# One program order over all stages, the second pass of a turn before its first down product, and another order of refill

## The chip, the cores and the metric

The kernel runs on one core of a Trainium2 chip. The metric is the device time of one execution in microseconds; lower is better. The input is fixed: 256 tokens, two layers.

## The reference

Each of the two layers does a token mixer and then a mixture of experts, both behind a root-mean-square norm and both added to the residual stream. Layer 0 mixes with differential attention, layer 1 with latent attention. The mixture picks for each token one group of eight and in it two of its eight experts; 64 experts per layer, each with three float32 matrices of 1024 x 256 or 256 x 1024 (1.049 MB each):

```python
for i in range(DEPTH):                       # 2
    h = rms_norm(x, attn_norm[i])
    x = x + (diff_attention if i == 0 else mla_attention)(h, ...)
    h = rms_norm(x, ffn_norm[i])
    x = x + hier_moe(h, ...)

def body(e, acc):                            # e = 0 .. 63
    hid = jax.nn.silu(t @ w_gate[e]) * (t @ w_up[e])
    return acc + combine[:, e, None] * (hid @ w_down[e])
```

## The kernel before

A layer is an attention stage (`diff_attention`, `latent_attention`), a front that norms, routes and sorts (`Front`), and the expert stage (`moe`). In the two attention stages and their fronts the instructions are written as named steps, and the strings `ORDER0` and `ORDER1` give the order in which they are issued.

The expert stage goes in 16 turns (0 to `LAST` = 15) of four experts. TensorE multiplies the four experts side by side, 32 columns each, so a pass has room for 32 tokens per expert (`SLOTS`). A pass consists of: the selection of tokens (`places`, DVE L1262), the gather by matrix products with the selection (`step`, TensorE L1270; `gained`, DVE L334), gate and up (`into`, `gate_up`, L1323), SiLU on ACT (L1328) and the product with up on DVE (L1330), the hidden columns transposed (L1335) and copied (ACT L1337), down (`out_of`, `down`, L1349), a copy out of PSUM (`taken`, L1381), and back (L1389), which spreads the rows over the tokens and adds them to `xs` (L1354). The weighted selection is transposed for it (`turned`, L1291). The product back of turn t is done in turn t + 1.

Where an expert has more than 32 tokens in a turn, the turn is full and takes a second pass. A word of bits, `path`, computed by the front, says which turns are full: `full` tests it (L1449, one If per turn, on every engine) and `second` is the body. Inside it, a further If (L1406) leads to `long_way`, for more than 64 tokens, which this input does not need. On this input three turns are full: turns 1 and 15 of layer 0 and turn 11 of layer 1.

Before, the If stands at the end of a turn, behind down, `taken` and the weighting for the next turn.

Weights pass through ten rooms of 2.1 MB. A unit of load is the gate and up of one expert (two DMAs), or the down matrices of two experts (two DMAs); three units per pair of experts, six per turn. Unit n lies in room n mod 10 of a ring (`RING`), so unit n + 10 can be loaded when unit n has been read for the last time. `load_unit` issues the DMAs on SP's queue, in the order of the list `order`; `free` marks units as read and issues the loads at the head of the list as long as their rooms are marked. The gate/up units are marked inside the If (in each of its branches), the down units behind it. SP issues in order, and each DMA waits there for the last reader of its room.

The planner keeps the written order of an engine's instructions only inside a `manual_schedule` region. Before, there are four such regions for TensorE, ACT and DVE: attention and front of layer 0 (`start`), the expert stage of layer 0, attention and front of layer 1 (`all_manual`), the expert stage of layer 1. What lies between two regions (`rope_tables` for layer 1, L264 to L267) and the order across an edge are the planner's. SP is in written order throughout.

TensorE's sequencer can be told ahead that a branch will probably be taken (`mark_branch_hint_location`): each If of a turn that is not full carries a hint for the If of the next turn. `preferred_fallthrough_block=True` puts the body of the If behind the branch, so that a turn that is not full jumps over `second`.

```python
order = list(range(ROOMS, 96 + 2 * ROOMS))
order[2:8] = order[3], order[4], order[2], order[6], order[7], order[5]
```

Of the kernel before, what the change touches and what calls it, by code (L numbers as in the profile page):

```python
# [10 lines left out]
F32R = mybir.dt.float32r  # L11
# [4 lines left out]
OP = mybir.AluOpType  # L16
# [53 lines left out]
def trunk_kernel(  # L70
# [14 lines left out]
    def psum_bank():  # L85
        return psum.tile([128, 512], F32, name="bank", bufs=8)
# [6 lines left out]
    def temp(cols):  # L93
        return work.tile([128, 512], F32, name="temp", bufs=3)[:, 0:cols]
# [140 lines left out]

    start = ctx.enter_context(ExitStack())
    start.enter_context(tc.manual_schedule(engines={e.engine for e in (PE, ACT, DVE, POOL, SP)}))
    ones_b = consts.tile([128, 128], BF, name="ones_b")
# [47 lines left out]
    def rsqrt_mean(r, ss, n, sq=None, plus=None, times=None, split=False, eps=EPS, rows=None):  # L286
# [29 lines left out]
        in_turns(newton)  # L316

    def all_manual():
        return tc.manual_schedule(engines={e.engine for e in (PE, ACT, DVE, POOL, SP)})

# [155 lines left out]
    def diff_attention():  # L476
# [265 lines left out]
        for name in ORDER0.split():  # L742
            steps[name]()
        start.close()
        return front


    def latent_attention():
# [330 lines left out]
        front = Front(1, step)  # L1079
        with all_manual():  # L1080
            for name in ORDER1.split():
                steps[name]()
        return front
# [210 lines left out]
    def moe(layer, front):  # L1294
# [30 lines left out]

        def hidden(gu, weight=None):
            sil, hid = temp(256), temp(256)
            ACT.activation(sil, gu[:, 0:256], AF.Silu)  # L1328
            if weight is None:
                DVE.tensor_mul(hid, sil, gu[:, 256:512])  # L1330
            else:
                DVE.scalar_tensor_tensor(hid, sil, weight, gu[:, 256:512], op0=OP.mult, op1=OP.mult)  # L1332
            tp = psum_bank()
            for k in range(2):
                PE.transpose(tp[:, 128 * k:128 * k + 128], hid[:, k::2], ident)  # L1335
            hdT = work.tile([128, 3, 128], F32, name="aT0")[:, 0:2, :]
            ACT.copy(hdT.rearrange("p k t -> p (k t)"), tp[:, 0:256])  # L1337
            return hdT
# [64 lines left out]

        def second(t, j, multiplied):

            with tc.If(path >> 16):  # L1406
                long_way(t, j)
            this = Gather(front, j)
            this.places(t, 1)
            this.rest()  # L1410
            this.weighted(t)
            gu = into(t, j)
            ACT.copy(selT[:, 1 - j], this.turned())
            multiplied()
            y = out_of(t, hidden(gu))
            back(taken(y, lambda: temp(512)), selT[:, 1 - j])
# [20 lines left out]
        order = list(range(ROOMS, 96 + 2 * ROOMS))  # L1437
        order[2:8] = order[3], order[4], order[2], order[6], order[7], order[5]
        state = {"next": 0, "free": set()}
        def full(t, path, done):  # L1440

            mark = dict(state)
# [6 lines left out]
            with tc.If((path >> t) & 1, preferred_fallthrough_block=True, label=f"full{layer}_{t}") as more:  # L1449
                second(t, t % 2 if t < LAST else (t + 1) % 2, at_once)  # L1450
            with more.Else():
# [3 lines left out]

        this, ts = front.first, None
        with tc.manual_schedule(engines={e.engine for e in (PE, ACT, DVE)}):
            for t in range(LAST + 1):
                g, _, pairs = halves_of(t)
                if t == LAST:  # L1460
                    back(ts, selT[:, (t + 1) % 2])
                    full(t, path, lambda: None)

                    rows, weight = temp(256).bitcast(F32R).rearrange("p (b t) -> p b t", b=2), small("sums", 1)
                    this.weighted(t, sel[:, (t + 1) % 2])
                    ACT.copy(rows, this.turned())
                    DVE.tensor_reduce(weight, this.turned(sel[:, (t + 1) % 2]), axis=AX.XY, op=OP.add)
                    y = out_of(t, hidden(into(t, t % 2), weight), 4, lambda y, n: back_last(y, n - 1, rows) if n else None)
                    back_last(y, 3, rows)
                    free(units(g, pairs, "gu") | units(g, pairs, "d"))  # L1470
                    break
                gu = into(t, t % 2)
                ACT.copy(selT[:, t % 2], this.turned())  # L1473
                if t:
                    back(ts, selT[:, (t + 1) % 2])
                hdT = hidden(gu)
                this = Gather(front, (t + 1) % 2)
                this.places(t + 1, 0)
                this.rest()
                y = out_of(t, hdT)  # L1480
                ts = taken(y, lambda: prob().rearrange("p a t -> p (a t)")[:, 0:512])
                if t + 1 < LAST:
                    this.weighted(t + 1)
                if t == 0:
                    path = nc.values_load(front.path[0:1, 0:1], min_val=0, max_val=2 ** 17 - 1)
                full(t, path, lambda: free(units(g, pairs, "gu")))
                free(units(g, pairs, "d"))

    moe(0, diff_attention())
# [79 lines left out]
```

## Time and profile before

| what | value |
|---|---|
| median of 3 runs | 1233.47 us (1233.05 to 1235.77) |
| the profiled execution | 1237.15 us, span 1235.3 us |
| TensorE busy | 996.9 us (81%) |
| VectorE (DVE) busy | 422.4 us (34%) |
| ScalarE (ACT) busy | 229.1 us (19%) |
| moved by DMA | 435.92 MB, mean 353 GB/s |
| mean granted TensorE clock | 0.924 |

The expert stage of layer 0 runs from about 155 to 656 us, that of layer 1 from about 767 to the end. Between them lies the attention of layer 1, before them that of layer 0. The table is a mean over all of these, which have different limits; what sets the time has to be read stage by stage.

### The profile page before, as it was taken

Reading aid. Unit: us, or ns where it says so; the run is one execution under the profiler, and the core shown is the slowest. Engines: PE = TensorE matmul, PEld = TensorE weight load, DVE = VectorE, ACT = ScalarE, POOL = GpSimd, SP = SyncE. Lnnn points to the kernel's source line nnn. Section 1 sums busy time; section 2 is a strip of 40 time slices with the busy share of each in tenths; the row PEclk is TensorE's granted clock in tenths of the full one; section 3 lists DMA queues with packets and bytes.
Section 4 is the critical chain, followed back from the end, with each engine's and each line's share of the span. In section 5 each row is a group of like instructions: output and inputs, shape, how many; then the busy total and the mean of one; then the engine's idle time right before and its main releaser. Section 6 shows DMA issues by size and latency. Waiting matters only on the chain. (4 is left out here: it accounts for less than half of the span.)

```text
span 1235.3 us, 16593 instructions
## 1 busy us (share of the span) xinstructions
PE 996.9 (81%) x6544; PEld 552.7 (45%) x6544; DVE 422.4 (34%) x996; ACT 229.1 (19%) x594; POOL 1.3 (0%) x23
## 2 busy tenths in 40 slices
PE   8998888777777777777888999787777777799776
PEld 8897744343333333333438777443233333343332
DVE  6897622221111111111318876222111111122122
ACT  5565410000000000000016874000000000001000
POOL 0000000000000000000000000000000000000000
PEclk9998999898988888888999999999888888899888
DMA  9456871999999999999943386999999999969994
GB/s 350 184 214 250 329 288 72 427 424 425 425 425 425 426 425 426 425 425 425 408 194 120 134 316 283 369 425 425 425 426 426 425 426 425 426 266 375 425 424 175
DMA packets 78007, 435.92 MB, mean 353 GB/s; under 512 B 6960, under 2 KB 23088, under 8 KB 30128
## 3 DMA queue, kind: packets, MB, share of 16 engines
q1 hardware_dynamic: 77728, 434.02, 85.2%
q8 instruction: 86, 1.41, 0.4%
q14 instruction: 49, 0.40, 0.1%
q10 hardware_dynamic: 144, 0.09, 0.0%
HBM read 433.03 MB, written 1.05 MB: 351 GB/s over the span
## 5 line engine op out<-in xcount | busy, mean ns | idle before, releaser
L1323 PE MATMUL bank<-room,areaC 128*32 128x512 f32 x2240 | 349.7, 701 | 154.2 <-DMA room<-in_moe_w_up_dram 108.3
L1323 PEld LDWEIGHTS bank<-room,areaC 128*32 128x32 f32 x2240 | 108.6, 126 | 389.9 <-issue 373.7
L1354 DVE TENSOR_TENSOR xs<-xs,bank 128x512 f32<-128x512 f32 (+1 forms) x148 | 96.9, 658 | 482.3 <-PE bank L1389 477.2
L1349 PE MATMUL bank<-room,aT 128*32 128x512 f32 (+1 forms) x1160 | 131.6, 583 | 2.5 <-ACT aT L1337 2.5
L1389 PE MATMUL bank<-prob,val 128*128 128x512 f32 x240 | 108.1, 593 | 1.9 <-DVEq L1449 1.9
L1473 ACT COPY val<-bank 128x256 f32<-128x256 f32 x30 | 11.2, 373 | 508.2 <-PE bank L1291 508.2
L422 PE MATMUL bank<-room,areaB 128*128 128x256 f32 (+3 forms) x544 | 86.6, 311 | 4.1 <-DVE room L390 2.7
L334 DVE TENSOR_TENSOR areaC<-bank,pack 128x512 f32<-128x512 f32 x70 | 48.4, 691 | 111.4 <-PE bank L1270 111.4
L422 PEld LDWEIGHTS bank<-room,areaB 128*128 128x128 f32 x544 | 76.3, 193 | 9.0 <-DVE room L390 3.2
L1270 PE MATMUL bank<-val,areaB 128*128 128x128 f32 x576 | 71.5, 284 | 7.6 <-PEq L1406 3.2
L1270 PEld LDWEIGHTS bank<-val,areaB 128*128 128x128 f32 x576 | 67.9, 197 | 10.7 <-issue 10.4
L1270 PE MATMUL bank<-val,areaA 128*128 128x128 f32 x544 | 66.9, 282 | 4.5 <-DVE lg L1182 1.9
L1349 PEld LDWEIGHTS bank<-room,aT 128*32 128x32 f32 x1160 | 35.3, 112 | 70.7 <-issue 62.0
L1270 PEld LDWEIGHTS bank<-val,areaA 128*128 128x128 f32 x544 | 63.6, 196 | 6.3 <-issue 6.0
L390 DVE TENSOR_TENSOR room<-room,room 128x2048 fp32r<-128x2048 f32 (+4 forms) x33 | 62.4, 1897 | 6.5 <-ACT room L388 6.5
L1389 PEld LDWEIGHTS bank<-prob,val 128*128 128x128 f32 x240 | 43.3, 190 | 46.7 <-issue 46.7
L388 ACT CAST room<-room 128x2048 fp32r<-128x2048 f32 (+4 forms) x33 | 51.9, 1589 | 16.7 <-PE bank L1323 8.0
L1381 DVE COPY prob<-bank 128x512 f32<-128x512 f32 x30 | 20.7, 691 | 87.3 <-PE bank L1349 87.3
L1335 PE MATMUL bank<-ident,temp 128*128 128x128 f32 x70 | 17.6, 334 | 40.5 <-DVE temp L1330 37.2
L1381 ACT COPY prob<-bank 128x512 f32<-128x512 f32 x30 | 17.6, 586 | 155.4 <-PE bank L1349 155.4
L422 PE MATMUL bank<-room,areaA 128*128 128x512 f32 (+1 forms) x176 | 43.9, 393 | 2.0 <-DVE areaA L692 2.0
L1335 PEld LDWEIGHTS bank<-ident,temp 128*128 128x128 f32 x70 | 11.0, 206 | 66.7 <-DVE temp L1330 61.5
(245 smaller groups left out, 748.7 us busy)
## 6 DMA issues: line engine op xcount, KB each, us to landing
room<-in_moe_w_gate_dram SPq DMA_DIRECT2D x124, 1024.0 KB, 17.8
room<-in_moe_w_up_dram SPq DMA_DIRECT2D x124, 1024.0 KB, 19.3
room<-in_moe_w_down_dram SPq DMA_DIRECT2D x122, 1024.0 KB, 19.6
room<-in_diff_w_in_dram SPq DMA_DIRECT2D x11, 1024.0 KB, 10.8
room<-in_diff_w_out_dram SPq DMA_DIRECT2D x2, 2048.0 KB, 9.3
room<-in_moe_w_gate_dram SPq DMA_DIRECT2D x8, 512.0 KB, 14.8
room<-in_moe_w_up_dram SPq DMA_DIRECT2D x8, 512.0 KB, 13.6
room<-in_moe_w_down_dram SPq DMA_DIRECT2D x8, 512.0 KB, 10.1
```

The source lines that it names most:

```text
L334: DVE.tensor_tensor(dst, tp, gain[:, k0:k0 + n, None].to_broadcast([128, n, dst.shape[2]]), op=OP.mult)
L388: step(c + name)(lambda f=f: f(hi().bitcast(F32R), w()))
L390: step(c + name)(lambda eng=eng: eng.tensor_tensor(lo().bitcast(F32R), w(), hi(), op=OP.subtract))
L422: PE.matmul(out, a[k][x_].bitcast(F32R), b[k][w_].bitcast(F32R), start=first and j == 0, stop=last and j == n - 1)
L1270: PE.matmul(self.ps[kk][:, k, :], self.front.xn[:, tb, 4 * kk + k, :], self.sel[:, tb, :], start=tb + k == 0, stop=tb == 1, skip_group_che ...
L1323: PE.matmul(gu[M * c:M * c + M], x(k, slice(M * c, M * c + M)), w[:, :, k, :], start=k == 0, stop=k == 7)
L1335: PE.transpose(tp[:, 128 * k:128 * k + 128], hid[:, k::2], ident)
L1349: PE.matmul(y[n][M * c:M * c + M], hdT[:, k, M * c:M * c + M], w[:, k, ns], start=first and k == 0, stop=last and k == 1, skip_group_check ...
L1354: DVE.tensor_add(xs[:, tb, ns], xs[:, tb, ns], acc)
L1381: (ACT.copy, DVE.tensor_copy)[n](t, y[n])
L1389: PE.matmul(acc, rows[:, tb, :], t, start=True, stop=True)
L1473: ACT.copy(selT[:, t % 2], this.turned())
```

## The change

All of TensorE, ACT, DVE and POOL stand in one `manual_schedule` region from the beginning, so every instruction is issued in written order, over the edges of the stages too.

In a turn the If now stands directly behind gate and up and the first two steps of hidden (`hidden_rows`: SiLU and the product), before the transposed selection, back, the hidden columns (`hidden_columns`), the gather of the next turn and down. The first hidden rows wait in 256 free columns of a `prob` tile (`held`) meanwhile. In a full turn the second pass so runs between the first gate/up and the first down. The test for the long way moves from the start of the second pass to behind its gate/up, becomes an If with an Else, and is hinted at the start of `second`; the gate/up units are marked as read in both branches. The word `path` is loaded into registers behind the first gate/up.

The list `order` is permuted in each of the first 14 turns: of the six units whose rooms a turn frees, the four in gate/up rooms are loaded first, the two in down rooms last. Before, only the beginning of the list was permuted, and in it unit 15 stood behind 16 and 17.

```diff
@@ -233,8 +233,7 @@
     b_rt = packed("router_bias").rearrange("p (l e) -> p l e", l=2)
 
 
-    start = ctx.enter_context(ExitStack())
-    start.enter_context(tc.manual_schedule(engines={e.engine for e in (PE, ACT, DVE, POOL, SP)}))
+    ctx.enter_context(tc.manual_schedule(engines={e.engine for e in (PE, ACT, DVE, POOL)}))
     ones_b = consts.tile([128, 128], BF, name="ones_b")
     DVE.memset(ones_b, 1.0)
     ident = consts.tile([128, 128], F32, name="ident")
@@ -315,9 +314,6 @@
             return newton
         in_turns(newton)
 
-    def all_manual():
-        return tc.manual_schedule(engines={e.engine for e in (PE, ACT, DVE, POOL, SP)})
-
     def square_x(tb):
         ss = work.tile([128, 1], F32, name="ss", bufs=2)
         ACT.activation(work.tile([128, D], BF, name="temp", bufs=3), xs[:, tb, :], AF.Square, accum_out=ss)
@@ -741,7 +737,6 @@
                     PE.matmul(idle[:, 0:128], ones_b, ones_b, start=True, stop=True)
         for name in ORDER0.split():
             steps[name]()
-        start.close()
         return front
 
 
@@ -1077,9 +1072,8 @@
             "Y": lambda: out_proj(oT[1], 0, [[t[:, j] for t in pair_b[0]] for j in range(2)]),
             "Z": lambda: out_proj(oT[1], 2, [[t[:, j] for t in pair_b[2]] for j in range(2)], order=X_LO_LAST)})
         front = Front(1, step)
-        with all_manual():
-            for name in ORDER1.split():
-                steps[name]()
+        for name in ORDER1.split():
+            steps[name]()
         return front
 
 
@@ -1323,13 +1317,19 @@
                     PE.matmul(gu[M * c:M * c + M], x(k, slice(M * c, M * c + M)), w[:, :, k, :], start=k == 0, stop=k == 7)
             return gu
 
-        def hidden(gu, weight=None):
-            sil, hid = temp(256), temp(256)
+        def hidden(gu, weight=None, hid=None):
+            return hidden_columns(hidden_rows(gu, weight, hid))
+
+        def hidden_rows(gu, weight=None, hid=None):
+            sil, hid = temp(256), temp(256) if hid is None else hid
             ACT.activation(sil, gu[:, 0:256], AF.Silu)
             if weight is None:
                 DVE.tensor_mul(hid, sil, gu[:, 256:512])
             else:
                 DVE.scalar_tensor_tensor(hid, sil, weight, gu[:, 256:512], op0=OP.mult, op1=OP.mult)
+            return hid
+
+        def hidden_columns(hid):
             tp = psum_bank()
             for k in range(2):
                 PE.transpose(tp[:, 128 * k:128 * k + 128], hid[:, k::2], ident)
@@ -1401,18 +1401,24 @@
                 add(tb, slice(w * n, w * n + w), acc)
                 stored(tb, slice(w * n, w * n + w))
 
-        def second(t, j, multiplied):
-
-            with tc.If(path >> 16):
-                long_way(t, j)
+        def second(t, multiplied):
+
+            j = (t + 1) % 2
+
+            tc.mark_branch_hint_location(f"long{layer}_{t}", "LikelyTaken", engines=[PE.engine])
             this = Gather(front, j)
             this.places(t, 1)
             this.rest()
             this.weighted(t)
-            gu = into(t, j)
+            hid = hidden_rows(into(t, j), None, held[1][:, 512:768])
+            with tc.If(path >> 16, preferred_fallthrough_block=True, label=f"long{layer}_{t}") as more:
+                long_way(t, j)
+                multiplied()
+            with more.Else():
+                multiplied()
+            hdT = hidden_columns(hid)
             ACT.copy(selT[:, 1 - j], this.turned())
-            multiplied()
-            y = out_of(t, hidden(gu))
+            y = out_of(t, hdT)
             back(taken(y, lambda: temp(512)), selT[:, 1 - j])
 
         def long_way(t, slot):
@@ -1435,10 +1441,14 @@
                     add(tb, ns, y[n])
 
         order = list(range(ROOMS, 96 + 2 * ROOMS))
-        order[2:8] = order[3], order[4], order[2], order[6], order[7], order[5]
+
+        for t in range(LAST - 1):
+            order[6 * t:6 * t + 6] = (order[6 * t + n] for n in (0, 1, 3, 4, 2, 5))
         state = {"next": 0, "free": set()}
         def full(t, path, done):
 
+
+
             mark = dict(state)
 
             def at_once():
@@ -1447,44 +1457,51 @@
                 done()
 
             with tc.If((path >> t) & 1, preferred_fallthrough_block=True, label=f"full{layer}_{t}") as more:
-                second(t, t % 2 if t < LAST else (t + 1) % 2, at_once)
+                second(t, at_once)
             with more.Else():
                 at_once()
                 if t < LAST:
                     tc.mark_branch_hint_location(f"full{layer}_{t + 1}", "LikelyTaken", engines=[PE.engine])
 
-        this, ts = front.first, None
-        with tc.manual_schedule(engines={e.engine for e in (PE, ACT, DVE)}):
-            for t in range(LAST + 1):
-                g, _, pairs = halves_of(t)
-                if t == LAST:
-                    back(ts, selT[:, (t + 1) % 2])
-                    full(t, path, lambda: None)
-
-                    rows, weight = temp(256).bitcast(F32R).rearrange("p (b t) -> p b t", b=2), small("sums", 1)
-                    this.weighted(t, sel[:, (t + 1) % 2])
-                    ACT.copy(rows, this.turned())
-                    DVE.tensor_reduce(weight, this.turned(sel[:, (t + 1) % 2]), axis=AX.XY, op=OP.add)
-                    y = out_of(t, hidden(into(t, t % 2), weight), 4, lambda y, n: back_last(y, n - 1, rows) if n else None)
-                    back_last(y, 3, rows)
-                    free(units(g, pairs, "gu") | units(g, pairs, "d"))
-                    break
-                gu = into(t, t % 2)
-                ACT.copy(selT[:, t % 2], this.turned())
-                if t:
-                    back(ts, selT[:, (t + 1) % 2])
-                hdT = hidden(gu)
-                this = Gather(front, (t + 1) % 2)
-                this.places(t + 1, 0)
-                this.rest()
-                y = out_of(t, hdT)
-                ts = taken(y, lambda: prob().rearrange("p a t -> p (a t)")[:, 0:512])
-                if t + 1 < LAST:
-                    this.weighted(t + 1)
-                if t == 0:
-                    path = nc.values_load(front.path[0:1, 0:1], min_val=0, max_val=2 ** 17 - 1)
-                full(t, path, lambda: free(units(g, pairs, "gu")))
+        def kept():
+            return prob().rearrange("p a t -> p (a t)")
+
+        this, ts, held = front.first, None, [kept() for _ in range(2)]
+        for t in range(LAST + 1):
+            g, _, pairs = halves_of(t)
+            weight = None
+            if t == LAST:
+                back(ts, selT[:, (t + 1) % 2])
+
+                weight = small("sums", 1)
+                this.weighted(t, sel[:, (t + 1) % 2])
+                DVE.tensor_reduce(weight, this.turned(sel[:, (t + 1) % 2]), axis=AX.XY, op=OP.add)
+            gu = into(t, t % 2)
+            hid = hidden_rows(gu, weight, held[0][:, 512:768])
+            if t == 0:
+                path = nc.values_load(front.path[0:1, 0:1], min_val=0, max_val=2 ** 17 - 1)
+            full(t, path, lambda: free(units(g, pairs, "gu")))
+            if t == LAST:
+                rows = temp(256).bitcast(F32R).rearrange("p (b t) -> p b t", b=2)
+                hdT = hidden_columns(hid)
+                ACT.copy(rows, this.turned())
+                y = out_of(t, hdT, 4, lambda y, n: back_last(y, n - 1, rows) if n else None)
+                back_last(y, 3, rows)
                 free(units(g, pairs, "d"))
+                break
+            ACT.copy(selT[:, t % 2], this.turned())
+            if t:
+                back(ts, selT[:, (t + 1) % 2])
+            hdT = hidden_columns(hid)
+            this = Gather(front, (t + 1) % 2)
+            this.places(t + 1, 0)
+            this.rest()
+            y = out_of(t, hdT)
+            held = [kept() for _ in y]
+            ts = taken(y, iter([h[:, 0:512] for h in held]).__next__)
+            if t + 1 < LAST:
+                this.weighted(t + 1)
+            free(units(g, pairs, "d"))
 
     moe(0, diff_attention())
     moe(1, latent_attention())
```

## Rows read from the trace of the kernel before

**Rows 1.** Busy time by stretch (us): engines, granted clock, DMA share, GB/s.

```profile
186.00:214.00 28.00, 23.36 (x182) 12.46 (x184) 8.38 (x15) 2.64 (x7) 0.00 (x0) 1.00 0.11 35
210.80:214.00 3.20, 1.48 (x14) 0.74 (x16) 0.42 (x1) 1.03 (x3) 0.00 (x0) 1.00 0.68 200
214.00:622.00 408.00, 313.57 (x1964) 135.38 (x1952) 83.68 (x142) 21.61 (x53) 0.00 (x0) 0.90 1.01 424
1098.00:1116.00 18.00, 14.82 (x132) 6.87 (x124) 3.88 (x8) 1.25 (x3) 0.00 (x0) 1.00 0.20 67
1116.00:1214.00 98.00, 77.90 (x480) 32.18 (x484) 24.17 (x40) 6.18 (x15) 0.00 (x0) 0.90 1.01 423
```

**Rows 2.** Timeline of TensorE, turn 11 of layer 1: start, duration, line [idle before].

```profile
1088.41 0.44 PE L1291 MATMUL bank<-ident,val 128*128 128x128 f32 x2
1088.69 3.60 PE L1389 MATMUL bank<-prob,val 128*128 128x512 f32 x8
...
1093.74 3.83 PE L1270 MATMUL bank<-val,areaA 128*128 128x128 f32 x32
1097.50 3.64 PE L1349 MATMUL bank<-room,aT 128*32 128x512 f32 x32
1103.04 3.81 PE L1270 MATMUL bank<-val,areaA 128*128 128x128 f32 x32 [1.90 <-PEq L1406]
1106.78 7.07 PE L1323 MATMUL bank<-room,areaC 128*32 128x512 f32 x64
1113.79 0.44 PE L1291 MATMUL bank<-ident,val 128*128 128x128 f32 x2
1115.43 0.50 PE L1335 MATMUL bank<-ident,temp 128*128 128x128 f32 x2 [1.20 <-DVE temp L1330]
1116.45 3.64 PE L1349 MATMUL bank<-room,aT 128*32 128x512 f32 x32 [0.52 <-ACT aT L1337]
```

**Rows 3.** Timeline of SP's queue: first expert load after the second pass of turn 1.

```profile
210.82 0.33 SPq L147 DMA_DIRECT2D room<-in_moe_w_gate_dram  x1
```

**Rows 4.** Who waited for whom: total us, times, longest; SP's queue, then TensorE.

```profile
SPq L147 <- PEq L1449: 155.1, 26, 14.3
...
PE bank L1335 <- DVE temp L1330: 37.2, 33, 1.3
...
PE bank L1323 <- DVEq L1449: 23.0, 17, 1.4
```

**Rows 5.** Timeline of TensorE: gate/up of turn 1, layer 0.

```profile
176.75 8.77 PE L1323 MATMUL bank<-room,areaC 128*32 128x512 f32 x64 [4.79 <-PEq L1449]
```

**Rows 6.** TensorE's branches, ns min/median/max: turn 0, turn 13, then all at L1406.

```profile
L1449 PEldq COMPARE_BRANCH  x1: 6247/6247/6247, 169.9 to 169.9; - x1
...
L1449 PEldq COMPARE_BRANCH  x1: 357/357/357, 1171.3 to 1171.3; - x1
...
L1406 PEldq COMPARE_BRANCH  x3: 3222/3892/5872, 195.9 to 1098.8; - x3
```

**Rows 7.** Timelines of TensorE, ACT and DVE around the end of layer 0.

```profile
604.78 3.67 PE L1389 MATMUL bank<-prob,val 128*128 128x512 f32 x8 [0.96 <-DVEq L1449]
...
644.27 3.51 PE L1349 MATMUL bank<-room,aT 128*32 128x256 f32 x32 [0.46 <-ACT aT L1337]
...
640.98 1.47 ACT L388 CAST room<-room 128x1536 fp32r<-128x1536 f32 x1 [7.96 <-PE bank L1323]
...
652.65 1.76 DVE L390 TENSOR_TENSOR room<-room,room 128x1536 fp32r<-128x1536 f32 x1 [0.32 <-ACT room L388]
...
656.70 0.69 DVE L334 TENSOR_TENSOR temp<-bank,pack 128x512 f32<-128x512 f32 x1 [0.43 <-PE bank L330]
```

**Rows 8.** Groups by line: busy us, mean ns; one of the rope tables' lines, layer 1.

```profile
L264 DVE SCALAR_TENSOR_TENSOR cos_t<-pack,pack 128x32 f32<-128x32 f32 x8 | 1.1, 182 | 0.0
```

**Rows 9.** Timeline of TensorE: the last turn of layer 1.

```profile
1211.59 1.08 PE L1291 MATMUL bank<-ident,val 128*128 128x128 f32 x4 [3.11 <-PEq L1449]
1212.61 9.50 PE L1323 MATMUL bank<-room,areaC 128*32 128x512 f32 x64
```

## The prediction

> **What bounds the kernel now.** I first read the slices of the page and cut the span into stages. Over most of both expert stages the DMA engines are full: 424 GB/s at a busy share of 1.01 from 214 to 622 us, 423 GB/s from 1116 to 1214 us [rows 1]. TensorE in the first stretch is busy 313.57 of 408 us. One turn loads 12 pieces of 1.049 MB, at 424 GB/s 29.7 us, and 313.57/408 of that is 22.8 us, so TensorE has 6.9 us to spare per turn. A step on TensorE there is worth nothing; what counts is when a room becomes free, and only where the DMA engines run dry.
>
> They run dry in two places. From 186 to 214 us they move 35 GB/s, from 1098 to 1116 us 67 GB/s [rows 1]. Against 424 GB/s that is 28 x (1 - 35/424) = 25.7 us and 18 x (1 - 67/424) = 15.2 us lost. Each lies in a turn that takes its second pass: layer 0 turn 1 and layer 1 turn 11 (the third, layer 0 turn 15, has no expert loads left behind it). TensorE's timeline of turn 11 [rows 2] shows why: gate/up ends at 1088.4 (E), then come back of the turn before, hidden, gather, down, and only then the second gather (1103.0) and the second gate/up, which ends at 1113.8 (E'). The gate/up rooms are read until then; refill starts 25.4 us after E. In layer 0 it is 210.82 [rows 3]; the DMAs regain full rate 3.2 x (1 - 200/424) = 1.7 us behind the issue (the short window of rows 1). So the queue was dry from 212.5 - 25.7 = 186.8 and, with the same 1.7 behind E', from 1115.5 - 15.2 = 1100.3.
>
> The queue of SP also waits 26 times, 155 us in all, for TensorE to pass the If [rows 4]: loads into down rooms cannot go before it. In the saturated stretches this is hidden by transfers in flight.
>
> **The change part by part.** *Second pass ahead of the first down.* It removes back, transposes, gather and down from between E and the second gather. It adds the wait for the first hidden rows and the selection: after gate/up, ACT's SiLU and DVE's product, for which the second pass's own transposes waited 1115.43 - 1113.79 = 1.6 us [rows 2], then DVE's branch and one selection; I take 2.2 us. Gather to gate/up is 1106.78 - 1103.04 = 3.74, gate/up 7.07 [rows 2]: E' = E + 13.0. Behind E': down starts at +2.66 (1116.45 - 1113.79), then down 3.6, second back 3.7, leaving the If with the last add 1.2, turned 0.4, back 3.6, transposes 0.4, gather 3.8, down 3.6 [rows 2]: the down rooms are free at about E' + 23.1.
>
> *Refill order.* Before, a turn's third load waits for a down room and holds two free gate/up rooms behind it. Now four units (8 pieces, 8.39 MB, 19.8 us at 424 GB/s) go at E or E', the other two when down has ended. In layer 0, unit 15 no longer stands behind units 16 and 17, which wait for turn 1: 2 pieces more (4.9 us) before the gap.
>
> Layer 1, turn 11: the queue still dries at 1100.3, resumes at 1088.4 + 13.0 + 1.7 = 1103.1 (2.8 lost), has work to 1122.9, then waits for down: 1101.4 + 23.1 + 1.7 = 1126.2 (3.3 lost). 15.2 - 6.1 = **9.1 us gained**.
> Layer 0, turn 1: gate/up ends at 185.5 now [rows 5]; by the same pieces it ends near 184.3 after, since the 4.79 us stall at the first If, the register load of `path` in it, moves from behind down to behind gate/up. Dry at 186.8 + 4.9 = 191.7, resumed at 184.3 + 13.0 + 1.7 = 199.0 (7.3 lost), dry at 218.8, down free 197.3 + 23.1, resumed 222.1 (3.3 lost). 25.7 - 10.6 = **15.1 us gained**. Later turns free rooms at least 9 us before the queue dries, so this lead is kept. Bounds for the two together: all 40.9, or 16 if a branch stall of 4 us stays exposed in each place where I have none.
>
> *If between gate/up and back, each turn.* What hides it are the 6.9 us. Gone are TensorE's waits for DVE at the hidden transposes (33 times, 37.2 us) and for DVE's passing of the If (17 times, 23.0 us) [rows 4], about 2.5 us a turn; added is the 1.6 us until DVE has the product and passes. With an exposed branch stall as at 176.75 (4.79) it would be +3.9, still covered. I take nothing; without the cover it is some 27 saturated turns times the excess.
>
> *Branches.* TensorE's branch over the second pass takes 6247 ns at turn 0, where no hint precedes, and 357 ns in a hinted turn; the jump over the long way takes 3222 to 5872 ns, three times [rows 6]. The change hints that jump, 13 us before it is reached. I count it as hidden, with 0 and 4 us as ends.
>
> [...]
>
> *One program order.* In the trace the planner has moved work over a region's edge at the end of layer 0. ACT's CAST for layer 1 (two of 1.47 us, the first at 640.98) stands before the last SiLU, DVE's 1.76 us product at 652.65 before the last corrections [rows 7]. In program order they come after. From the end of down(14) (back could start 0.96 before 604.78): back 3.7, weighted and turned 1.7, gate/up 7.1, then 2.2 + 3.7 + 7.1 + 2.7 + 3.6 + 3.7 for the second pass, 1.2 to leave, 1.1 to down: 641.6 against 644.27, 2.7 gained; then 1.3 and 1.4 for the second CAST and the product. The last add ends near 650.9; the two CASTs fill ACT to 651.8, the product DVE to 653.6, and the first step of layer 1, now 656.70 [rows 7], can start there: **3.1 us gained**, bounds 0 and 5.4.
>
> The rope tables of layer 1 (16 small DVE instructions of about 0.18 us, 8 on one row [rows 8]) now lie in gaps of attention 0; they come behind the front, where DVE is idle under the first gate/up (7 us). Removed 0 to 2.9, added 0: I take 0, as the dependent instructions around them leave such gaps.
>
> *End of layer 1.* TensorE waits 3.11 us at the last If before the last gate/up [rows 9], because the hint came too late; after the change a whole turn lies between hint and branch. Gate/up could start near 1209.6 instead of 1212.61, but the DMAs are full to 1214 [rows 1], and the last four down halves (2.1 MB, 5 us) go last: the last gate/up pieces land near 1210. **1.5 us gained**, bounds 0 and 3.1.
>
> Sum: 15.1 + 9.1 + 3.1 + 1.5 = 28.8 us. The profiled execution took 1237.15 us (span 1235.3), so 1208.4; the median of the runs is 3.7 lower: 1233.47 - 28.8 = 1204.7. I say 1205, on its own 1198 to 1213.
>
> **Rivals.** [...]
> *B: no drying at all.* If TensorE needs less than I give it in the second pass: 25.7 + 15.2 + 4.6 = 45.5, 1188. Against: turn 0's stall and rows 2.
> *C: slower, TensorE becomes the bound.* Place: the If behind gate/up, where TensorE now waits for ACT, DVE and the branch in every turn. It decides once more than 6.9 us are added to a turn, and outweighs 28.8 us from 6.9 + 28.8/27 = 8.0. At 9 us: 27 x 2.1 - 28.8 = +28, 1261. Against: 3.9 is what rows 4 and 5 give with every branch unhinted. [...]
> *D: no effect.* The idle is found again before the next stage, as in a front that waits for something else: 1233. Against: layer 1's start hangs on the last add of layer 0 [rows 7].
>
> **How the numbers follow.** Forecast 0.62, A 0.19, B 0.08, C 0.07, D 0.04. Faster by over 0.2% (2.5 us, about what can be told from no change): 0.62 + 0.19 + 0.08 = 0.89; same 0.04; slower 0.07. Range 1193 to 1222: it takes in A, half of what lies towards B, not C and D.
>
> **What would show it.** Right: from 186 to 214 us DMA well above 35 GB/s with two short holes, likewise near turn 11; SP's loads there waiting for gate/up, not 25 us behind E; TensorE's long-way branches below 1 us; CAST behind the last add of layer 0. Wrong: the saturated stretch below 420 GB/s, TensorE without DMA waits there (C), or as many dry microseconds in other turns (A, D).

## The result, and the profile after

The changed kernel takes 1190.72 us (median of 4 runs, 1189.34 to 1192.82), the kernel before beside it 1233.26. The ratio is 0.9653 with a 95% interval of 0.9631 to 0.9675: 42.5 us gained, where 28.8 were forecast. 1190.7 lies 2.3 us below the lower end of the range. The direction and the places were right, the sizes too small.

The page of the changed kernel: its span, busy time by engine, and the moved GB/s in 40 slices of the span.

```profile
span 1187.9 us, 16711 instructions
...
PE 970.6 (82%) x6544; PEld 544.0 (46%) x6544; DVE 425.8 (36%) x996; ACT 232.0 (20%) x594; POOL 1.3 (0%) x23
...
GB/s 353 203 210 261 353 255 363 383 425 426 425 425 425 426 425 425 426 426 426 412 220 141 136 311 300 354 426 425 426 426 426 426 425 426 425 424 378 424 426 263
```

The work is the same, 6544 matmuls on TensorE before and after. TensorE is busy 970.6 us for 996.9, at a mean granted clock of 0.935 for 0.924; DVE and ACT are busy 3 us longer. These means do not say where the gain lies; the stages do. The same places as in [rows 1], from the changed kernel (columns as there: length, busy time of TensorE, its weight loads, DVE, ACT and POOL, granted clock, DMA share, GB/s):

```profile
184.00:192.00 8.00, 6.60 (x65) 1.84 (x54) 0.96 (x3) 0.39 (x1) 0.00 (x0) 1.00 0.61 218
192.00:208.00 16.00, 14.25 (x76) 7.08 (x77) 6.70 (x11) 1.98 (x5) 0.00 (x0) 1.00 0.99 415
208.00:216.00 8.00, 8.00 (x79) 3.39 (x81) 2.24 (x4) 0.59 (x1) 0.00 (x0) 1.00 0.73 268
...
224.00:576.00 352.00, 269.27 (x1697) 116.88 (x1697) 74.08 (x125) 21.32 (x50) 0.00 (x0) 0.90 1.01 425
...
1068.00:1076.00 8.00, 6.51 (x60) 1.94 (x52) 0.42 (x1) 1.62 (x4) 0.00 (x0) 1.00 0.90 359
1076.00:1092.00 16.00, 14.55 (x84) 8.08 (x84) 7.91 (x12) 1.33 (x3) 0.00 (x0) 1.00 1.01 425
1092.00:1096.00 4.00, 4.00 (x44) 1.22 (x40) 1.02 (x2) 0.00 (x0) 0.00 (x0) 1.00 0.59 195
```

Each long dry stretch has become two short holes, as forecast. Against 424 GB/s, layer 0 loses 8 x (1 - 218/424) + 16 x (1 - 415/424) + 8 x (1 - 268/424) = 7.1 us where it lost 25.7, layer 1 1.2 + 2.2 = 3.4 us where it lost 15.2. Between 224 and 576 us the DMA engines stay full and TensorE is busy 269 of 352 us, so the If in each turn costs nothing.

TensorE's timeline of the changed kernel, turns 0 and 1 of layer 0, then turn 11 of layer 1 (to be read beside [rows 2, 5]; in brackets how long the engine was idle before the row and what ended that, PEq being TensorE's own sequencer):

```profile
160.73 0.41 PE L1285 MATMUL bank<-ident,val 128*128 128x128 f32 x2 [1.98 <-PEq L1459]
...
171.21 7.05 PE L1317 MATMUL bank<-room,areaC 128*32 128x512 f32 x64
179.64 3.84 PE L1264 MATMUL bank<-val,areaB 128*128 128x128 f32 x32 [1.37 <-DVE val L1256]
183.40 7.07 PE L1317 MATMUL bank<-room,areaC 128*32 128x512 f32 x64
...
212.97 7.05 PE L1317 MATMUL bank<-room,areaC 128*32 128x512 f32 x64
...
1049.86 8.54 PE L1317 MATMUL bank<-room,areaC 128*32 128x512 f32 x58 [3.91 <-DMA room<-in_moe_w_up_dram]
1059.66 3.84 PE L1264 MATMUL bank<-val,areaA 128*128 128x128 f32 x32 [1.27 <-DVE val L1256]
1063.43 7.07 PE L1317 MATMUL bank<-room,areaC 128*32 128x512 f32 x64
1071.69 0.47 PE L1335 MATMUL bank<-ident,prob 128*128 128x128 f32 x2 [1.19 <-DVEq L1414]
...
1092.78 7.05 PE L1317 MATMUL bank<-room,areaC 128*32 128x512 f32 x64
```

The second gather follows the first gate/up by 1.4 us in layer 0 and 1.3 us in layer 1. SP's queue issues at the ends of these blocks, not 25 us behind the first:

```profile
190.49 0.34 SPq L147 DMA_DIRECT2D room<-in_moe_w_gate_dram  x1
...
213.16 0.33 SPq L147 DMA_DIRECT2D room<-in_moe_w_gate_dram  x1
```

At 190.49 the second gate/up has just ended; at 213.16 the down products of both passes are done, which is the wait for down rooms. The waits of the changed kernel (SP's, then TensorE's) show the queue behind the If down from 155.1 us [rows 4] to 30.2 + 14.4:

```profile
SPq L147 <- PE bank L1349: 67.4, 8, 17.6
...
SPq L147 <- PEq L1414: 30.2, 2, 16.6
...
SPq L147 <- PEq L1459: 14.4, 5, 4.9
```

```profile
PE bank L1285 <- PEq L1459: 13.9, 5, 4.5
```

TensorE's branches in the changed kernel (ns min/median/max): the first If, the last If, and the three over the long way (compare [rows 6]).

```profile
L1459 PEldq COMPARE_BRANCH  x1: 3590/3590/3590, 156.7 to 156.7; - x1
...
L1459 PEldq COMPARE_BRANCH  x1: 345/345/345, 1171.4 to 1171.4; - x1
...
L1414 PEldq COMPARE_BRANCH  x3: 336/345/366, 187.8 to 1067.9; - x3
```

A hinted If is not always short: those of turns 6 and 7 of layer 0 took 4872 and 4026 ns in this trace, under transfers of 420 to 425 GB/s.

The edge of the layers in the changed kernel, on ACT and DVE: both CASTs for layer 1 now stand behind ACT's last correction of layer 0 (623.51), the product (626.66) behind the last add to `xs` (625.48), while in [rows 7] one CAST stands ahead of the last SiLU and the product ahead of the last corrections. The first step of layer 1 starts at 628.34.

```profile
623.51 0.37 ACT L406 CAST prob<-bank 128x256 fp32r<-128x256 f32 x1 [1.29 <-PE bank L1349]
623.78 2.85 ACT L384 CAST room<-room 128x1536 fp32r<-128x1536 f32 x2
...
625.48 0.75 DVE L1354 TENSOR_TENSOR xs<-xs,bank 128x256 f32<-128x256 f32 x2 [0.48 <-PE bank L1400]
626.66 1.76 DVE L386 TENSOR_TENSOR room<-room,room 128x1536 fp32r<-128x1536 f32 x1 [0.43 <-ACT room L384]
628.34 1.28 DVE L330 TENSOR_TENSOR temp<-bank,pack 128x512 f32<-128x512 f32 x2
```

The last turn of layer 1, TensorE of the changed kernel: the 3.11 us wait of [rows 9] is gone, and gate/up takes 7.66 us for 9.50.

```profile
1166.86 7.66 PE L1317 MATMUL bank<-room,areaC 128*32 128x512 f32 x64
1175.66 0.47 PE L1335 MATMUL bank<-ident,prob 128*128 128x128 f32 x2 [1.14 <-DVEq L1459]
```

Cut at the same places of the program, the two profiled executions compare as follows (us of span, from TensorE's gate/up rows):

| stage | before | after | gained | forecast |
|---|---|---|---|---|
| A: to the first gate/up of layer 0 | 155.2 | 151.6 | 3.6 | 0 |
| B: to the end of gate/up, turn 14 | 436.0 | 417.8 | 18.2 | 15.1 |
| C: to the first gate/up of layer 1 | 175.5 | 169.2 | 6.3 | 3.1 |
| D: to the end of gate/up, turn 11 | 321.8 | 319.8 | 2.0 | 0 |
| E: to the end of gate/up, turn 14 | 102.7 | 89.6 | 13.1 | 9.1 |
| F: to the end | 44.1 | 39.9 | 4.2 | 1.5 |

### The profile page after: what moved, and what is told of

It is laid out like the page before. It is cut to its first block, busy times and chain, and to the rows that moved or that the text cites. A ratio compares the mean times of both kernels' runs of the same rounds, so it can differ in the third digit from the quotient of the medians.

```text
span 1187.9 us, 16711 instructions
## 1 busy us (share of the span) xinstructions
PE 970.6 (82%) x6544; PEld 544.0 (46%) x6544; DVE 425.8 (36%) x996; ACT 232.0 (20%) x594; POOL 1.3 (0%) x23
## 5 line engine op out<-in xcount | busy, mean ns | idle before, releaser
L1317 PE MATMUL bank<-room,areaC 128*32 128x512 f32 x2240 | 332.0, 675 | 105.2 <-DMA room<-in_moe_w_up_dram 105.2
L1317 PEld LDWEIGHTS bank<-room,areaC 128*32 128x32 f32 x2240 | 97.0, 123 | 329.8 <-issue 314.5
L1327 DVE TENSOR_TENSOR prob<-temp,bank 128x256 f32<-128x256 f32 x33 | 13.9, 422 | 385.9 <-ACTq L1459 192.8
L1349 PE MATMUL bank<-room,aT 128*32 128x512 f32 (+1 forms) x1160 | 128.3, 572 | 1.2 <-ACT aT L1337 1.2
L1389 PE MATMUL bank<-prob,val 128*128 128x512 f32 x240 | 111.3, 607 | 3.1 <-issue 2.0
L1325 ACT ACTIVATE temp<-bank 128x256 f32<-128x256 f32 x35 | 13.4, 384 | 481.7 <-PE bank L1317 481.7
L1264 PE MATMUL bank<-val,areaB 128*128 128x128 f32 x576 | 75.2, 292 | 18.8 <-DVE val L1256 15.2
L1264 PEld LDWEIGHTS bank<-val,areaB 128*128 128x128 f32 x576 | 71.3, 205 | 24.6 <-DVE val L1256 17.4
L1264 PE MATMUL bank<-val,areaA 128*128 128x128 f32 x544 | 66.9, 282 | 16.3 <-DVE val L1256 13.7
L1389 PEld LDWEIGHTS bank<-prob,val 128*128 128x128 f32 x240 | 44.5, 196 | 50.6 <-issue 49.0
L1381 DVE COPY prob<-bank 128x512 f32<-128x512 f32 x30 | 20.8, 692 | 89.4 <-PE bank L1349 89.4
L1285 PE MATMUL bank<-ident,val 128*128 128x128 f32 x74 | 15.5, 292 | 44.8 <-DVEq L1459 28.0
```

The costliest lines, as they stand in the source:

```text
L1264: PE.matmul(self.ps[kk][:, k, :], self.front.xn[:, tb, 4 * kk + k, :], self.sel[:, tb, :], start=tb + k == 0, stop=tb == 1, skip_group_che ...
L1285: PE.transpose(tp[:, tb, :], (self.sel if sel is None else sel)[:, tb, :], ident)
L1317: PE.matmul(gu[M * c:M * c + M], x(k, slice(M * c, M * c + M)), w[:, :, k, :], start=k == 0, stop=k == 7)
L1349: PE.matmul(y[n][M * c:M * c + M], hdT[:, k, M * c:M * c + M], w[:, k, ns], start=first and k == 0, stop=last and k == 1, skip_group_check ...
L1381: (ACT.copy, DVE.tensor_copy)[n](t, y[n])
L1389: PE.matmul(acc, rows[:, tb, :], t, start=True, stop=True)
```

## The experiments

Four questions were open: how much of the 47.4 us between the two spans is the change and how much one execution against another; how the gain divides over the three parts (place of the second pass, refill order, one program order); whether the hint makes the jump over the long way short; and whether the holes that are left wait for down rooms. Ratios are to the kernel before, with 95% intervals.

**The kernel before, once more**, with no edit.

> The kernel before, unchanged, for a second profile of it. Layer 0's first gate/up began 3.6 us earlier in the profile after (151.6 against 155.2 us), of which 2.6 us arise before 27 us of the span, where nothing was changed. Theory 1 (a late landing in that one execution): this profile has layer 0's first gate/up near 152 to 153 us and takes 1233 us. Theory 2 (the moved rope tables and the order are worth it): again near 155 us.

Measured: 1233.68 us in one run, span 1231.9. A is 148.9, D 319.8, E 108.0; B, C and F as before within 0.7. Over all thirteen profiled executions A lies between 148.2 and 155.2, although nothing in it was changed but the region and, in one kernel, a hint. So the 3.6 us in A and the 2.0 in D are one execution against another, not the change. E varies with one branch, over the long way in turn 11: 3.9 us in the first trace, here

```profile
L1406 PEldq COMPARE_BRANCH  x1: 7245/7245/7245, 1090.1 to 1090.1; - x1
```

of which the second gather waited 5.43 us, against 1.90 in [rows 2], and then took 5.58 us itself, against 3.81:

```profile
1097.70 5.58 PE L1270 MATMUL bank<-val,areaA 128*128 128x128 f32 x32 [5.43 <-PEq L1406]
```

The two differences, 3.5 and 1.8 us, are the whole 5.3 us. In the five traces with the old place of the second pass this wait is 1.90, 2.94, 3.04, 3.71 and 5.43 us, and E is 102.7, 104.9, 105.0, 106.1 and 108.0 us in the same order. The first trace had the shortest.

**The changed kernel, once more**, with no edit.

> The changed kernel, unchanged, as the yardstick for the three beside it and for a second profile of it: 1191 us.

Measured: 1188.83, 0.9620 [0.9588, 0.9652]; stages B to F within 0.1 us of the first trace, A 3.2 shorter. The table's gains in B, C and F are the change's; that in E is too, but its size hangs on the execution of the kernel before, from 13.1 to 18.4 us.

**One region alone.**

```diff
-    start.enter_context(tc.manual_schedule(engines={e.engine for e in (PE, ACT, DVE, POOL, SP)}))
+    ctx.enter_context(tc.manual_schedule(engines={e.engine for e in (PE, ACT, DVE, POOL)}))
...
-        with all_manual():
...
-        with tc.manual_schedule(engines={e.engine for e in (PE, ACT, DVE)}):
```

> The kernel before with the one program order alone; turns and refill as before. Theory 1 (as priced: the moved CASTs and product at the end of layer 0 are worth 3 us net, the rope tables nothing): 1230 us. Theory 2 (the order is worth more, 8 us or so, since the time gained beyond the sum lies at the stages' edges): 1225 us. Rival (program order costs in the attention stages): over 1233 us.

Measured: 1230.12, 0.9963 [0.9940, 0.9986]. C is 172.5 instead of 175.5: 3.0 us, with the CASTs behind ACT's last correction and the product behind the last add. Theory 1 holds.

**The change with the four regions of before.**

```diff
-    ctx.enter_context(tc.manual_schedule(engines={e.engine for e in (PE, ACT, DVE, POOL)}))
+    start.enter_context(tc.manual_schedule(engines={e.engine for e in (PE, ACT, DVE, POOL, SP)}))
...
+        with all_manual():
...
+        with tc.manual_schedule(engines={e.engine for e in (PE, ACT, DVE)}):
```

> The changed kernel with the four regions of before. Theory 1: 3 us are given back, 1194 us. Theory 2: 8 us, 1199 us. If the planner now moves work between the new turns' parts and the attention of layer 1, more.

Measured: 1192.73, 0.9655 [0.9623, 0.9688], 2.0 to 3.9 above the two medians of the changed kernel; the intervals overlap, so the time alone does not tell. Its trace does: C is 172.1 against 169.2, and on DVE the product for layer 1 stands before the last add again:

```profile
626.00 1.76 DVE L390 TENSOR_TENSOR room<-room,room 128x1536 fp32r<-128x1536 f32 x1 [0.32 <-ACT room L388]
628.77 0.85 DVE L1360 TENSOR_TENSOR xs<-xs,bank 128x256 f32<-128x256 f32 x2 [0.67 <-PE bank L1406]
```

**The refill order alone, in the kernel before.**

```diff
-        order[2:8] = order[3], order[4], order[2], order[6], order[7], order[5]
+
+        for t in range(LAST - 1):
+            order[6 * t:6 * t + 6] = (order[6 * t + n] for n in (0, 1, 3, 4, 2, 5))
```

> The kernel before with the new refill order alone. Theory (it moves only unit 15 ahead of the gap in turn 1 of layer 0, 4.9 us; the gate/up rooms of a full turn are as late as before): 1229 us. Rival (the order is worth the 20 us by itself that taking it out of the changed kernel costs): 1214 us.

Measured: 1234.62, 0.9991 [0.9967, 1.0014]: nothing gained, against the theory. B is 4.4 us shorter, since turn 1's dry stretch shrinks to 24 x (1 - 57/424) = 20.8 us, but C is 6.9 longer. The trace shows where most of these are: the second pass of turn 15 took 4.6 us longer than in the repeated run of before and the last gather ahead of layer 1's first gate/up 1.7 us, with a granted clock of 0.65 from 600 to 605 us and 0.50 from 757 to 764 us. These two windows, then TensorE's second gather and down of turn 15 and that last gather:

```profile
600.00:605.00 5.00, 2.85 (x13) 2.88 (x14) 0.43 (x1) 0.00 (x0) 0.00 (x0) 0.65 1.04 382
...
757.00:764.13 7.13, 6.40 (x32) 5.98 (x31) 2.07 (x10) 0.00 (x0) 0.00 (x0) 0.50 0.30 124
```

```profile
602.15 6.73 PE L1270 MATMUL bank<-val,areaB 128*128 128x128 f32 x32 [3.14 <-PEq L1406]
...
618.54 5.30 PE L1349 MATMUL bank<-room,aT 128*32 128x512 f32 x32 [0.52 <-ACT aT L1337]
...
760.45 3.75 PE L1270 MATMUL bank<-val,areaA 128*128 128x128 f32 x16 [0.73 <-DVE temp L1243]
```

In the repeated run of before the same three took 3.81, 3.64 and 2.02 us, the first of them after a wait as long (in the first trace of before it took 3.81 us too, at clock 1.00 behind 3.16 us):

```profile
604.74 3.81 PE L1270 MATMUL bank<-val,areaB 128*128 128x128 f32 x32 [3.20 <-PEq L1406]
```

Why the clock fell here stays open.

**The change with the old order.**

```diff
-
-        for t in range(LAST - 1):
-            order[6 * t:6 * t + 6] = (order[6 * t + n] for n in (0, 1, 3, 4, 2, 5))
+        order[2:8] = order[3], order[4], order[2], order[6], order[7], order[5]
```

> The changed kernel with the refill order of before. Theory (the order is what keeps the queue fed from the second gate/up to the end of down): in turn 1 of layer 0 the queue dries 4.9 us earlier and has 6 pieces instead of 8 behind the second gate/up (4.9 us), in turn 11 of layer 1 it has 4 pieces instead of 8 (9.9 us): 1191 + 20 = 1211 us, with DMA holes of that size behind the second gate/up. Rival (only the earlier release of the gate/up rooms counts; my sum gave the order 4.9 us): 1196 us.

Measured: 1210.15, 0.9803 [0.9770, 0.9836]: 19 to 21 us above the changed kernel. B is 425.5 and E 101.7 (after: 417.8 and 89.6). In turn 11 the gate/up rooms come free as early as after, but loads for down rooms stand in front of theirs, and the second hole is long:

```profile
1068.00:1076.00 8.00, 6.84 (x65) 2.12 (x56) 0.93 (x3) 0.38 (x1) 0.00 (x0) 1.00 0.92 373
1076.00:1092.00 16.00, 14.26 (x77) 7.09 (x76) 6.97 (x11) 1.98 (x5) 0.00 (x0) 1.00 0.66 275
1092.00:1096.00 4.00, 4.00 (x40) 2.06 (x42) 0.94 (x2) 0.58 (x1) 0.00 (x0) 1.00 0.01 4
```

The last two rows lose 5.6 + 4.0 us, and the hole goes on until the next load of gate/up at 1096.89; in the changed kernel the same 20 us lose 2.2.

**The place of the second pass alone.**

```diff
-    ctx.enter_context(tc.manual_schedule(engines={e.engine for e in (PE, ACT, DVE, POOL)}))
+    start.enter_context(tc.manual_schedule(engines={e.engine for e in (PE, ACT, DVE, POOL, SP)}))
...
+        with all_manual():
...
-
-        for t in range(LAST - 1):
-            order[6 * t:6 * t + 6] = (order[6 * t + n] for n in (0, 1, 3, 4, 2, 5))
+        order[2:8] = order[3], order[4], order[2], order[6], order[7], order[5]
...
+        with tc.manual_schedule(engines={e.engine for e in (PE, ACT, DVE)}):
```

> The changed kernel with the old refill order and the four regions: the new place of the If and of the second pass alone. Theory (the place frees the gate/up rooms early, but without the order the queue has 6 and 4 pieces instead of 8 behind them; e3 gave 1210, the regions 3 us): 1213 us. Rival (regions and refill hinder each other, so that the place alone brings the most): under 1205 us.

Measured: 1211.17, 0.9820 [0.9780, 0.9860]: 22 to 23 us gained, near the theory's 1213.

**Order and region without the new place** (the edit is against the kernel before).

```diff
-    start.enter_context(tc.manual_schedule(engines={e.engine for e in (PE, ACT, DVE, POOL, SP)}))
+    ctx.enter_context(tc.manual_schedule(engines={e.engine for e in (PE, ACT, DVE, POOL)}))
...
-        with all_manual():
...
-        order[2:8] = order[3], order[4], order[2], order[6], order[7], order[5]
+
+        for t in range(LAST - 1):
+            order[6 * t:6 * t + 6] = (order[6 * t + n] for n in (0, 1, 3, 4, 2, 5))
...
-        with tc.manual_schedule(engines={e.engine for e in (PE, ACT, DVE)}):
```

> The kernel before with the new refill order and one program order, the If and the second pass where they were. Theory (order alone shortens one hole by 4.8 us and gave that back between the layers, where the planner filled the edge otherwise; with one program order it is kept): 1230 - 4.8 = 1225 us. Rival (the order is worth nothing without the earlier second pass): 1230 us.

Measured: 1229.18, 0.9948 [0.9925, 0.9971], hardly below the region alone, against the theory. B is 5.0 us shorter than with the region alone and C 6.4 longer; the second gather in turn 15 took 6.68 us and the last gather ahead of layer 1 3.75, as with the order alone. So the order by itself gains 4 to 5 us in B and loses 6 to 7 at the edge of the layers, most of it in these slower gathers; in the medians it is worth 0 to 2 us. Beside the new place it is worth about 20 us, and the new place without it 22: both are needed for the 42. All eight combinations of the three parts have now been run.

**The change without the hint for the long way.**

```diff
-            tc.mark_branch_hint_location(f"long{layer}_{t}", "LikelyTaken", engines=[PE.engine])
```

> The changed kernel without the hint for the jump over the long way. Theory (the jump then takes 3 to 7 us on TensorE behind the second gate/up, some 2 us of it under the gate/up; in turns 1 and 11 the down rooms come free that much later, in turn 15 of layer 0 the end of the layer does): 3 to 5 us for each of three places, 1201 us. Rival (hidden behind the wait for the second hidden rows): 1191 us.

Measured: 1191.04, 0.9638 [0.9607, 0.9669]: no difference. The three branches over the long way, unhinted:

```profile
L1413 PEldq COMPARE_BRANCH  x3: 434/458/4060, 184.6 to 1064.7; - x3
```

Two are short without a hint; behind the one of 4060 ns (turn 15) TensorE waited 1.80 us, and C is hardly longer (169.6 for 169.2). E is 1.9 us longer than in the repeated run, 1.7 of it in the last gate/up before its end (8.72 us for 7.03), far from the jump. In the new place the jump is mostly short or covered, and in this trace it is so without the hint.

**Down ahead of back and of the next gather.** If the holes wait for down rooms, TensorE should do down first in each turn.

```diff
+            hdT = hidden_columns(hid)
             ACT.copy(selT[:, t % 2], this.turned())
+            y = out_of(t, hdT)
+            free(units(g, pairs, "d"))
+            this = Gather(front, (t + 1) % 2)
+            this.places(t + 1, 0)
             if t:
                 back(ts, selT[:, (t + 1) % 2])
-            hdT = hidden_columns(hid)
-            this = Gather(front, (t + 1) % 2)
-            this.places(t + 1, 0)
-            this.rest()
-            y = out_of(t, hdT)
             held = [kept() for _ in y]
             ts = taken(y, iter([h[:, 0:512] for h in held]).__next__)
+            this.rest()
             if t + 1 < LAST:
                 this.weighted(t + 1)
-            free(units(g, pairs, "d"))
```

> The changed kernel with down of a turn right behind the If, ahead of back of the turn before and of the gather for the next, so that the down rooms of a full turn come free some 7 us earlier. Theory (the DMA holes before down has ended, 2.9 us in turn 1 of layer 0 and 2.2 in turn 11 of layer 1, cost their length): 1186 us and no hole there. Rival (the lead is lost elsewhere, or TensorE's turn gets longer than it can hide): 1191 us or more.

Measured: 1181.74, 0.9565 [0.9534, 0.9596]: faster than both kernels, 7 to 9 us below the changed one. The windows of this kernel:

```profile
184.00:192.00 8.00, 6.28 (x60) 2.02 (x56) 0.42 (x1) 1.03 (x3) 0.00 (x0) 1.00 0.51 176
192.00:208.00 16.00, 15.45 (x91) 6.45 (x84) 6.84 (x11) 1.92 (x4) 0.00 (x0) 1.00 1.01 423
208.00:216.00 8.00, 8.00 (x75) 4.05 (x77) 1.99 (x4) 0.00 (x0) 0.00 (x0) 1.00 1.01 426
...
1092.00:1096.00 4.00, 1.25 (x12) 0.13 (x4) 0.42 (x1) 0.38 (x1) 0.00 (x0) 0.91 1.01 422
```

The second hole is gone in both places (208 to 216 us: 426 GB/s for 268; 1092 to 1096: 422 for 195); the first, which waits for E', is still there. B is 3.2 us shorter than after, E 1.9, C 0.8. B and E together are the 5.1 us of the two holes, as the theory had it; the rest of the 7 to 9 us is C and one execution against another.

**The same, with two more hints**, for the If of turn 0 and for the If behind each full turn (the edit beyond the one just shown).

```diff
+                tc.mark_branch_hint_location(f"full{self.layer}_0", "LikelyTaken", engines=[PE.engine])
...
+            if t < LAST:
+                tc.mark_branch_hint_location(f"full{layer}_{t + 1}", "LikelyTaken", engines=[PE.engine])
```

> Down first as in e7, and TensorE hints for the If of turn 0 (given in the front) and for the If behind a full turn (given behind the long-way test). Theory (the unhinted branch of turn 0 took 3.6 us and left TensorE idle for 2.0; turn 1 of layer 0, where the DMA queue runs dry, would come 0.6 us earlier, the branches behind full turns lie under full DMAs): 1181 us, no difference from e7 that can be told. Rival (turns 2 and 12 set the pace after a full turn): 4 us for each, 1174 us.

Measured: 1188.28, 0.9624 [0.9593, 0.9654]: 6.5 us slower than without them. The 3.6 us branch of turn 0 is gone, and gate/up of turn 1 comes 1.0 us sooner. The Ifs behind the full turns, now hinted, still take 5.8 and 6.0 us. The last If, whose own hint is unchanged, now takes 5.9 us instead of 0.35. That branch, and TensorE behind it:

```profile
L1462 PEldq COMPARE_BRANCH  x1: 5927/5927/5927, 1166.8 to 1166.8; - x1
```

```profile
1173.12 0.67 PE L1336 MATMUL bank<-ident,prob 128*128 128x128 f32 x2 [3.03 <-PEq L1462]
```

F is 44.5 us instead of 39.8, as in the kernel before, whose last If took 6.1 us. From 1166 to 1176 and from 1176 to 1186 us the granted clock is 0.82 and 0.84, in the changed kernel 1.00 in both. This prices F's gain: it is this one branch, with the slower matmuls behind its wait. E is 2.1 us longer too, since the second gather of turn 11 stood still between two of its matmuls, for 2.66 us in which the profile shows nothing that it waited for:

```profile
1061.40 0.72 PE L1265 MATMUL bank<-val,areaA 128*128 128x128 f32 x5 [2.66 <-issue]
```

Why added hints go with a long branch elsewhere is not shown.

## Why the prediction was too small

The four terms of the sum were 3.1, 4.0, 3.2 and 2.7 us too small, 13.0 of the 13.7 us that were missed. The mechanism, the early release of the gate/up rooms and the refill in that order, came as written.

**Where the queue runs dry: right.** Both holes, their places, the wait for down rooms as the second of them, and the early refill came as forecast. E' = E + 13.0 was E + 12.2 in layer 0 and E + 12.1 in layer 1, since the wait taken as 2.2 us was 1.4 and 1.3. The down rooms, put at E' + 23.1, were free at about E' + 22.5 in both layers.

**Layer 0, turn 1: 15.1 forecast, 18.2 measured.** The step that failed is "it ends near 184.3 after, since the 4.79 us stall at the first If [...] moves". From the first gate/up to E it took 185.5 - 155.2 = 30.3 us before, I forecast 29.1, and it took 178.3 - 151.6 = 26.7. The stall did not move whole: the branch took 3590 ns, not 6247, and 1.98 us of it was exposed. And gate/up of turn 1 took 7.05 us, not 8.77: before, it followed that idle time at a granted clock of 0.50, as this window of the kernel before shows, then 0.93 and 1.00.

```profile
176.50:179.50 3.00, 2.75 (x14) 1.87 (x18) 0.00 (x0) 0.00 (x0) 0.00 (x0) 0.50 1.02 431
```

In all five traces with the old place this gate/up took 8.65 to 9.10 us behind a wait of 4.49 to 4.79, in all eight with the new place 7.05 to 7.07. I priced the stall by its idle time and not by the slow matmuls behind it. With E 2.4 us and E' another 0.8 nearer, the first hole is 4.2 us instead of 7.3.

**Layer 1, turn 11: 9.1 forecast, 13.1 measured.** Dry time fell by 15.2 - 3.4 = 11.8, 2.7 more than forecast: the holes of 2.8 and 3.3 were 1.2 and 2.2, as E' and the end of down came sooner. The other 1.3 us of E are not located. The term also rests on one trace of the kernel before, in which the stall at the long way happened to be at its shortest: 1.90 us exposed, 5.43 in the next execution, against which E's gain is 18.4.

**The edge of the layers: 3.1 forecast, 6.3 measured.** One program order gives 3.0, shown from both sides (alone 3.0, taken out 2.9). The other 3.3 come with the new turns: the gather of turn 15's second pass waited 3.16 us for its branch before and starts 1.42 us behind gate/up now. The mis-sized steps are the sum from the end of down(14) to the start of the last down, 37.8 us forecast and 35.4 measured, and the rest up to layer 1's first step, 12.0 forecast and 10.2 measured. The rope tables were not tried by themselves.

**The end of layer 1: 1.5 forecast, 4.2 measured.** The step "the last gate/up pieces land near 1210" failed as a limit: gate/up ran from 1166.86 to 1174.5 while the DMA engines were full, and waited for no load. It starts 2.5 us sooner in its stage, and is 1.8 us shorter; before, it began at a granted clock of 0.50 (1212 to 1214 us). What F gained is the branch. Nor is the late hint, which the prediction gives as the cause, enough: in the last experiment that branch took 5.9 us with its hint a whole turn ahead.

**Refill order.** Forecast as 4.9 us for two pieces and as part of the early issue; the runs show that without it about 20 of the 42 us are lost.

**The If in each turn, and rival C: 0, right.** The loads run at 425 GB/s between 224 and 576 us. Of TensorE's five waits for its own sequencer at the If (13.9 us, the longest 4.5) two stand at turn 0 of a layer and three in later turns under transfers of 420 GB/s and more. The second hole, put at 3.3 us in each place, was real at 2.9 and 2.2 us; down first removes it. **Rival B** named nearly the right time, 1188, by luck and without the mechanism: the holes did not vanish. **D** is refuted by the stages.

**Hints.** "I count it as hidden" came true, but the cause given, the hint, is not needed for it. In the changed kernel's trace most of TensorE's jumps over the second pass took 0.33 to 0.46 us, six took 3.6 to 6.6 us, and five lie between, at 0.6 to 2.3 us. No run here shows what the long ones wait for, or which branch will be long.

The four terms sum to 41.8 (18.2 + 6.3 + 13.1 + 4.2), against 42.5 between the medians. That close a match is partly luck: the second traces of both kernels give 17.4 + 6.3 + 18.4 + 4.4 = 46.5, where their runs give 45.3 between the medians.

## What to carry to other kernels

A refill order and the place of the work that frees its rooms are one change: measure them together, since here the order alone gave 0 to 2 us, the place alone 22, and both together 41 to 42. A stall of TensorE costs its idle time and can cost slow matmuls behind it as well: here 4.79 us, and behind it 8.77 us of gate/up for 7.05. Where it waits for a branch, one trace is too few to price it: the same wait was 1.90 us in one trace and 5.43 in another. Where the DMA queue runs dry, look which room its head waits for, and move that room's last reader forward.

## What the runs showed of the hardware

The same branch in the same program took 3.9 and 7.2 us in two executions. The same gather behind the same wait of 3.1 to 3.2 us took 3.81 us in one kernel and 6.73 in another that differs only in the order of its loads. The granted clock was 1.00 over the fast one in the first trace of before, and 0.65 from 600 to 605 us, where the slow one began. With two more branch hints the kernel took 6.5 us longer.
